# 3x3 convs one after the other on VectorE, read from PSUM, in a hybrid SSD and ConvFFN layer

## The chip, the cores and the metric

The kernel runs on one core of a Trainium2 chip. The core has TensorE for matmuls (PE in the profile, PEld for its weight loads), VectorE (DVE), ScalarE (ACT), GpSimd (POOL) and SyncE (SP), which here issues the DMAs. Matmul results land in PSUM; SBUF holds everything else. The metric is the device time of one execution in microseconds, lower is better.

## What is computed

One layer of a diffusion backbone runs over 640 tokens: 512 latent tokens, which form a grid of 8 rows by 64, and 128 context tokens. The model width is 1024. First comes a token mixer (a bidirectional state-space scan beside a 31-tap conv, one output projection), then a gated ConvFFN, where the change lies:

```python
h = rms_norm(x, prm["norm_ffn_pre"]) * (1 + sc2) + sh2
up = h @ prm["w_ffn_up"]                       # 1024 -> 5632
# context: width-3 conv along the sequence; latent: 3x3 conv on the grid, depthwise
up = dwconv1d(...) if rows is None else dwconv2d(up, prm["w_ffn_conv"], prm["b_ffn_conv"], rows)
f_gate, f_val = jnp.split(up, 2, axis=-1)
f = (jax.nn.silu(f_gate) * f_val) @ prm["w_ffn_down"]   # 2816 -> 1024
x = x + g2 * rms_norm(f, prm["norm_ffn_post"])
```

All arrays are float32.

## The kernel before

Activations lie transposed: 128 channels on the partitions, the 640 tokens along the free dimension, so that a tile is 128 x 640. Float32 matmuls are made of three products: weight and activation are each split into a rounded part (`hi`) and the rest (`lo`), and `mm3` (L267) adds hi x hi, hi x lo and lo x hi. Each product takes two matmuls, of 384 and 256 columns, so that one chunk of 128 output channels, with 8 blocks of 128 input channels, is 48 matmuls. Weights come by DMA in units of 512 KB (`fetch`), ScalarE writes their `hi` (L165) and GpSimd their `lo` (L167), two units ahead; there are three buffers for each part.

The up projection has 44 chunks. Number i stands for pair q = i // 2 and its half, gate (even) or value (odd). A chunk's sums fill one of three PSUM buffers in turn (`next_ps`), so that a chunk can start only when the one three before has been read to its end. Reading it is the conv, `up_conv`: ScalarE writes centre tap plus bias into a slot in SBUF (L1069), and VectorE adds the eight other grid taps (L1079, 441, 448 or 504 elements by tap) and the two taps of the context tokens (L1081, L1082; 127 elements), ten instructions that each read and write the same slot. When both halves of a pair are done, `finish(q)` applies SiLU to the gate (ScalarE, L1155) and multiplies it with the value (GpSimd; L1157 for the first four pairs, which are split into hi and lo at once, L253 and L255, and L1161 for the others, which are kept whole in the slots of `FRAW`). When the last chunk's matmuls are done, `split_f` splits what was kept (L253 on ScalarE, L255 on VectorE), into the slots of `ht`, some of which held the up projection's own input until then. The down projection follows.

The first five chunks, the head, are special. The activations come in two column ranges, 0 to 383 early and 384 to 639 late (`all_h2`). Chunks 0, 1 and 2 take their first range into the three PSUM buffers; chunks 3 and 4 take theirs into the free part of two of these, and ScalarE copies it to SBUF (L1104, `raws`, slots H5 and H6). When the second range is there, the order is 0, 3, 4, 1, 2 (L1101); chunks 3 and 4 are again copied to SBUF.

In the kernel before, six chunks (1, 2, 5, 6, 15 and 16; the table `EV`) are copied by ScalarE from PSUM to SBUF as soon as they are there (L1131), and their conv reads the copy, so that the PSUM buffer is free after the copy. The convs of chunks 3 and 4, from SBUF too, come behind those of chunks 8 and 14.

The framework orders each engine's instructions when the program is built, by a simulation of the timeline with priority by program order; each engine then works through its list in that order and waits on semaphores. Two instructions on one engine can therefore be swapped or mixed where the simulation saw the earlier one wait. `tc.issue_after(ins)` keeps what is traced inside it behind `ins` on the engine of `ins`. In the kernel before it binds the convs of chunks 0, 1 and 2 to one order, and those of 3 and 4 behind their forerunners; the others are free.

Of the kernel before, what the change touches and what calls it, by code (L numbers as in the profile page):

```python
# [9 lines left out]
AF = mybir.ActivationFunctionType  # L10
# [7 lines left out]
T = L + C  # L18
# [3 lines left out]
KD = D // P  # L22
# [7 lines left out]
NF = DFF // P  # L30
# [17 lines left out]
def hybrid_layer_kernel(ctx: ExitStack, tc: tile.TileContext, xT, ct, prm, cst, wrest, wdt, idhl_d, wada1, wada2, win,  # L48
                        wout, wup, wdown, st0, yT, nsf, nsb):
    nc = tc.nc  # L50
    te, ve, ac, gp, sy = nc.tensor, nc.vector, nc.scalar, nc.gpsimd, nc.sync
# [81 lines left out]
    def fetch(upto):  # L133
        if horizon[0] is not None:
            upto = min(upto, horizon[0])
        while cursor[0] < len(units) and cursor[0] <= upto:
            j = cursor[0]
            src, _ = units[j]
            n = src.shape[1]
            t = wp.tile([P, 1024], F32, tag="wr", name=f"wr{j}", bufs=2)  # L140
            sy.dma_start(t[:, :n], src)
            loaded[j] = t
            cursor[0] += 1
            split_unit(j)

    def get_unit(i):
        fetch(i + AHEAD)
        return ready.pop(i)
# [86 lines left out]
    ups = [(q, half) for q in range(NF) for half in range(2)]  # L235
# [25 lines left out]
    def mm3(pt, hi, lo, j, xh, xl, first, last, halves=(0, 1)):  # L261
        w1 = hi[:, j * P:(j + 1) * P]
        w2 = lo[:, j * P:(j + 1) * P]
        for i, (w, x) in enumerate(((w1, xh), (w1, xl), (w2, xh))):
            for h in halves:
                o, c0, c1 = HALF[h]
                last_mm[0] = te.matmul(pt[:, o:o + c1 - c0], w, x[:, c0:c1], start=first and i == 0, stop=last and i == 2)  # L267
# [28 lines left out]
    def ada_load(i, tags):  # L296
        ws = []
        for kc, tag in enumerate(tags):
            t = slot(tag)
            sy.dma_start(t[:, 0:4 * P], wada2[i, kc])  # L300
            ws.append(t)
        return ws

    def ada_half(i, ws):
        pt = psq(i % 2)
        for kc, w in enumerate(ws):
            for j in range(4):
                te.matmul(pt[32 * j:32 * j + 32, 0:P], cts[:, kc, :], w[:, j * P:(j + 1) * P],
                          start=kc == 0, stop=kc == KD - 1, tile_position=(0, 32 * j))
        r = sm.tile([P, P], F32, tag="adar", name=nm("adar"), bufs=1)  # L310
        ac.activation(r, pt[:, 0:P], AF.Copy)
        b = 8 * ADA_REST[i // 2] + 4 * (i % 2)
        ada_out(r, pt, P, (b, b + 1, b + 2, b + 3))
# [457 lines left out]
    for it in seq:  # L771
        if it[0] == "proj":
            n = it[1]
            pt = proj(n)
# [86 lines left out]
    prior = None  # L861
    for p in range(NA, NPAIR):
        for h in range(2):
            with tc.issue_after(prior.ins) if prior else nullcontext():
                prior = ve.scalar_tensor_tensor(tp[p][:, h * HT:(h + 1) * HT], tp[p][:, h * HT:(h + 1) * HT],
                                                prm_col("ssd_g", p), pry[h][:, 0:HT], MUL, MUL)
# [11 lines left out]
    def next_ps():  # L878
        rot[0] += 1
        return psum(rot[0] % 3)  # L880
# [169 lines left out]
    for half in range(2):  # L1050
        for m in range(OUT_FULL, KD):
            pt = next_ps()
# [14 lines left out]
    def up_conv(v, i, out):  # L1067
        w = lambda a, b: prm_col("ffn_w", 9 * i + 3 * a + b)
        ac.activation(out, v, AF.Identity, bias=prm_col("ffn_b", i), scale=w(1, 1))  # L1069
        vl = v[:, 0:L].rearrange("p (r c) -> p r c", c=GW)  # L1070
        ol = out[:, 0:L].rearrange("p (r c) -> p r c", c=GW)
        for a in range(3):
            for b in range(3):
                if (a, b) == (1, 1):
                    continue
                r0, r1 = max(0, 1 - a), min(ROWS, ROWS + 1 - a)
                q0, q1 = max(0, 1 - b), min(GW, GW + 1 - b)
                ob = ol[:, r0:r1, q0:q1]
                ve.scalar_tensor_tensor(ob, vl[:, r0 + a - 1:r1 + a - 1, q0 + b - 1:q1 + b - 1],  # L1079
                                        w(a, b), ob, MUL, ADD)  # L1080
        ve.scalar_tensor_tensor(out[:, L + 1:T], v[:, L:T - 1], w(1, 0), out[:, L + 1:T], MUL, ADD)  # L1081
        return ve.scalar_tensor_tensor(out[:, L:T - 1], v[:, L + 1:T], w(1, 2), out[:, L:T - 1], MUL, ADD)  # L1082
# [8 lines left out]
    head = [next_ps() for i in range(3)]  # L1091
    raws = {i: slot(f"H{2 + i}") for i in range(3, HEAD)}
# [5 lines left out]
    def up_mm(i, k, half, pt, o):  # L1098
        (hi, lo), (c0, c1) = ws[i], HC[half]
        for j, (w, x) in enumerate(((hi, h2[k][0]), (hi, h2[k][1]), (lo, h2[k][0]))):  # L1100
            te.matmul(pt[:, o:o + c1 - c0], w[k] if i in (1, 2) else w[:, k * P:(k + 1) * P], x[:, c0:c1],  # L1101
                      start=k == 0 and j == 0, stop=k == KD - 1 and j == 2)
        if k == KD - 1 and i >= 3:
            ac.activation(raws[i][:, c0:c1], pt[:, o:o + c1 - c0], AF.Copy)  # L1104
# [17 lines left out]
    conved = {}  # L1122


    EV = {1: "S14", 2: "S15", 5: "S6", 6: "S7", 15: "S14", 16: "S15"}

    def up_conv_of(i, v, out):
        conved[i] = out
        if i in EV:
            raw = slot(EV[i])  # L1130
            ac.activation(raw, v, AF.Copy)  # L1131
            v = raw
        return up_conv(v, ups[i][1] * NF + ups[i][0], out)

    acc_slot = lambda q, half: slot({(1, 0): "S16", (2, 1): "S17"}.get((q, half), f"S{10 + 2 * half + q % 2}"))
    ada_half(6, ada_w2)
    prior = None
    for i in (0, 3, 4, 1, 2):
        if i >= 3:
            pt = psq((i + 1) % 2)  # L1140
            for k in range(KD):
                up_mm(i, k, 1, pt, 0)
            horizon[0] += 1
            fetch(horizon[0])
            continue
        with tc.issue_after(prior.ins) if prior else nullcontext():
            for k in range(KD):
                up_mm(i, k, 1, head[i], 512)
            prior = up_conv_of(i, view(head[i]), acc_slot(*ups[i]))
    horizon[0] = None  # L1150
    FRAW = [f"H{i}" for i in (2, 3, 4, 7, 0, 5, 1, 6, 8, 9, 10, 11, 12, 13, 14, 15)] + ["S8", "S9"]

    def finish(q):
        a, b = conved.pop(2 * q), conved.pop(2 * q + 1)
        ac.activation(a, a, AF.Silu)  # L1155
        if q < NDIR:
            gp.tensor_tensor(a, a, b, MUL)  # L1157
            f_hl[q] = split_act(f"S{2 * q}", f"S{2 * q + 1}", a, gp)
        else:
            f_raw[q] = slot(FRAW[q - NDIR])  # L1160
            gp.tensor_tensor(f_raw[q], a, b, MUL)  # L1161

    finish(0)
    for i in range(HEAD, 2 * NF):
        q, half = ups[i]
        w = get_unit(unit_of["up", i])
        pt = next_ps()
        for k in range(KD):
            mm3(pt, *w, k, *h2[k], k == 0, k == KD - 1)
        if i == 2 * NF - 1:  # L1170
            break
        prior = up_conv_of(i, view(pt), acc_slot(q, half))
        if half and q > 2:
            finish(q)
        if i in (8, 14):
            j = 3 if i == 8 else 4
            with tc.issue_after(prior.ins):
                up_conv_of(j, raws[j], slot(f"H{j - 3}"))
            finish(j // 2)
        if i == 11:  # L1180
            with tc.issue_after(last_mm[0].ins):
                ada_half(7, ada_w2)
        if i == 5:
            ada_w2 = ada_load(7, [f"H{8 + k}" for k in range(8)])


    ht = ([(f"T{i}", f"T{8 + i}") for i in range(8)] + [("H2", "H3"), ("H4", "H7"), ("H0", "H5"), ("H1", "H6")]
          + [(f"S{i}", f"S{i + 1}") for i in (10, 12, 14)] + [(f"H{i}", f"H{i + 1}") for i in (8, 10, 12)])
    def split_f(q):
        f_hl[q] = split_act(*ht[q - NDIR], f_raw[q], ve)  # L1190

# [8 lines left out]
    gg2 = sb.tile([P, KD, 2], F32, tag="asc", name="gg2")  # L1200
    ve.tensor_tensor(gg2, modv[:, 40:48, :], prm_col("g_ffn_post", 0, 8).unsqueeze(2).to_broadcast([P, 8, 2]), MUL)
    msq = sb.tile([P, T], F32, tag="ysq", name="m2sq")
    mtags = ["H14", "H15", "S8", "S9", "S16", "S17", "U0", "U1"]
    mg = [None] * KD
    def down_mm(m, half, pt, ks):
        halves = BOTH if half is None else (half,)
# [61 lines left out]
    for m in range(2, KD - 1):  # L1268
        pt = next_ps()
# [4 lines left out]
    pt = next_ps()  # L1274
    down_mm(m, 0, pt, range(NF))
    down_out(m, 0, pt)
    pt = next_ps()
# [131 lines left out]
```

## Time and profile before

| | |
|---|---|
| median of three runs | 1042.57 us (1042.2 to 1050.46) |
| profiled execution, device time | 1052.25 us |
| profiled execution, span | 1050.5 us |
| granted TensorE clock, mean over the span | 0.979 |
| busy: PE, DVE, POOL, ACT | 94%, 73%, 55%, 42% |
| up chunks after the head | 575.4 to 876.3 us of the span |

How to read the lines below. A row of a group gives the line, the engine and the operation, output <- inputs (`ps` and `pq` are PSUM tiles, `S`, `H`, `T` slots in SBUF, `wr`, `wh`, `wl` the raw, hi and lo weights, `prms` the table of parameters), shapes and count, then busy time in us and mean ns of one, then the idle time of the engine ahead of these instructions and what ended most of it. A row of the timeline has the start and the time taken in us, merged over the count at its end, and in brackets the idle time ahead and its releaser. A row of the waits says who waited for whom: us in total, times, the longest. A row of the windows has the stretch, its length, and for PE, PEld, DVE, ACT and POOL the busy us and the instructions, then the granted TensorE clock, the share of the DMA engines and GB/s.

### The profile page before, as it was taken

What the parts mean: (1) busy time and instruction counts of PE and PEld (TensorE: products, weight loads), DVE (VectorE), ACT (ScalarE), POOL (GpSimd) and SP (SyncE); (2) the same over time, 40 slices, a digit from 0 to 9 for tenths busy, and PEclk for the clock granted to TensorE, in tenths of its full rate; (3) what the DMA queues carried; (4) which work ended last, traced back from release to release, by engine and by line L of the source; (5) the groups of instructions that cost most, each with busy time, mean ns of one, the idle gap of its engine ahead of it and who ended that gap; (6) DMA issues with size and microseconds to landing.
All of it is one profiled execution on the core that took longest, in us unless ns stands there. A gap on an engine that the chain in (4) does not pass through costs nothing. (4 is left out here: it accounts for less than half of the span.)

```text
span 1050.5 us, 18797 instructions
## 1 busy us (share of the span) xinstructions
PE 985.3 (94%) x7655; PEld 950.9 (91%) x7655; DVE 767.6 (73%) x1125; ACT 442.8 (42%) x740; POOL 573.5 (55%) x402
## 2 busy tenths in 40 slices
PE   5999999999999899799989968989999999999996
PEld 2799999999899789799879968989999999999995
DVE  3789999989999988942585999998888889300004
ACT  6244648556365676423455422333233235222221
POOL 3333978879769875443662434574443444344444
PEclk9999999999999999899999989999999999899998
DMA  9622221222111122478462311221222222132212
GB/s 346 221 66 76 66 71 61 71 75 69 60 61 48 36 59 80 159 268 287 134 210 96 118 41 61 61 80 61 81 67 75 81 63 68 56 88 65 71 54 101
DMA packets 42934, 102.76 MB, mean 98 GB/s; under 512 B 4832, under 2 KB 12768, under 8 KB 42848
## 3 DMA queue, kind: packets, MB, share of 16 engines
q1 hardware_dynamic: 42848, 101.56, 29.8%
q8 instruction: 60, 0.98, 0.4%
q14 instruction: 26, 0.21, 0.1%
HBM read 97.87 MB, written 3.67 MB: 97 GB/s over the span
## 5 line engine op out<-in xcount | busy, mean ns | idle before, releaser
L167 POOL TENSOR_TENSOR wl<-wr,wh 128x1024 fp32r<-128x1024 f32 (+3 forms) x127 | 301.2, 2373 | 318.2 <-ACT wh L165 312.2
L267 PE MATMUL ps<-H,wh 128*128 128x384 f32 (+1 forms) x1664 | 327.1, 310 | 4.9 <-DVE M L413 2.2
L267 PE MATMUL ps<-T,wh 128*128 128x384 f32 (+1 forms) x1504 | 287.9, 312 | 17.8 <-DVE S L1082 17.7
L165 ACT ACTIVATE wh<-wr 128x1024 fp32r<-128x1024 f32 (+3 forms) x131 | 131.7, 1005 | 351.2 <-PE ps L267 232.1
L267 PEld LDWEIGHTS ps<-H,wh 128*128 128x128 f32 x1664 | 253.3, 188 | 9.0 <-issue 4.3
L267 PEld LDWEIGHTS ps<-T,wh 128*128 128x128 f32 x1504 | 229.8, 190 | 18.7 <-issue 18.4
L1079 DVE SCALAR_TENSOR_TENSOR S<-ps,prms,S 128x441 f32<-128x441 f32 (+2 forms) x288 | 197.4, 693 | 34.3 <-ACT S L1069 28.0
L713 DVE SCALAR_TENSOR_TENSOR ps<-u,prms,ps 128x655 f32<-128x655 f32 x223 | 200.8, 901 | 9.9 <-ACT ps L710 5.4
L267 PE MATMUL ps<-H,wl 128*128 128x384 f32 (+1 forms) x832 | 198.1, 310 | 0.0
L267 PE MATMUL ps<-T,wl 128*128 128x384 f32 (+1 forms) x752 | 174.3, 311 | 0.0
L267 PEld LDWEIGHTS ps<-H,wl 128*128 128x128 f32 x832 | 130.8, 188 | 1.8 <-issue 1.4
L267 PEld LDWEIGHTS ps<-T,wl 128*128 128x128 f32 x752 | 117.1, 190 | 0.0
L333 DVE RECIPROCAL rsm<-rsm 128x160 f32<-128x160 f32 (+2 forms) x9 | 7.3, 815 | 143.8 <-ACT rsm L332 143.8
L267 PE MATMUL ps<-S,wh 128*128 128x384 f32 (+1 forms) x448 | 96.4, 323 | 7.5 <-DVE S L1082 3.2
L267 PEld LDWEIGHTS ps<-S,wh 128*128 128x128 f32 x448 | 73.6, 197 | 10.0 <-issue 5.9
L267 PE MATMUL ps<-S,wl 128*128 128x384 f32 (+1 forms) x224 | 58.7, 315 | 0.3 <-POOL wl L167 0.3
L629 ACT ACTIVATE S<-pq,ACM 128x128 f32<-128x128 f32 x140 | 40.9, 372 | 18.3 <-PE pq L623 18.1
L1079 DVE SCALAR_TENSOR_TENSOR S<-S,prms,S 128x441 f32<-128x441 f32 (+2 forms) x48 | 46.0, 988 | 1.4 <-ACT S L1069 1.3
L267 PEld LDWEIGHTS ps<-S,wl 128*128 128x128 f32 x224 | 38.1, 193 | 0.5 <-POOL wl L167 0.5
L1069 ACT ACTIVATE S<-ps,prms 128x640 f32<-128x640 f32 x36 | 31.3, 868 | 0.0
L1161 POOL TENSOR_TENSOR H<-S,S 128x640 f32<-128x640 f32 x16 | 25.5, 1594 | 3.9 <-DVE S L1082 3.8
L580 POOL TENSOR_TENSOR S<-S,stmp 128x128 f32<-128x128 f32 x36 | 18.6, 517 | 15.1 <-ACT S L569 11.2
(345 smaller groups left out, 1245.1 us busy)
## 6 DMA issues: line engine op xcount, KB each, us to landing
wr<-in_wup SPq DMA_DIRECT2D x44, 512.0 KB, 3.4
wr<-in_win SPq DMA_DIRECT2D x36, 512.0 KB, 3.4
T<-in_wada SPq DMA_DIRECT2D x49, 256.0 KB, 5.4
wr<-in_wdown SPq DMA_DIRECT2D x16, 512.0 KB, 3.5
wr<-in_wout SPq DMA_DIRECT2D x13, 512.0 KB, 3.5
H<-in_wada SPq DMA_DIRECT2D x23, 256.0 KB, 5.1
S<-in_wada SPq DMA_DIRECT2D x16, 256.0 KB, 5.7
wr<-in_wdown SPq DMA_DIRECT2D x8, 384.0 KB, 3.1
```

The lines of the kernel that those rows point to most:

```text
L165: ac.activation(hi[:, :n], raw[:, :n], AF.Copy)
L167: lo_eng.tensor_tensor(lo[:, :n], raw[:, :n], hi[:, :n].bitcast(F32), SUB)
L267: last_mm[0] = te.matmul(pt[:, o:o + c1 - c0], w, x[:, c0:c1], start=first and i == 0, stop=last and i == 2)
L333: ve.reciprocal(r[:, 0:seg], r[:, 0:seg])
L580: gp.tensor_tensor(now, now, tmp, ADD)
L629: ac.activation(r[:, c * P:(c + 1) * P], pb[:, (c - c0) * P:(c - c0 + 1) * P], AF.Relu, scale=-1.0, bias=ACM[:, c, row:row + 1])
L713: ve.scalar_tensor_tensor(acc, u[:, j:j + UO], w(j), acc, MUL, ADD)
L1069: ac.activation(out, v, AF.Identity, bias=prm_col("ffn_b", i), scale=w(1, 1))
L1079: ve.scalar_tensor_tensor(ob, vl[:, r0 + a - 1:r1 + a - 1, q0 + b - 1:q1 + b - 1], w(a, b), ob, MUL, ADD)
L1161: gp.tensor_tensor(f_raw[q], a, b, MUL)
```

## The change

`EV` and its copies go: every conv reads its chunk from PSUM, but for chunks 3 and 4, whose sums lie in `raws`. Every conv's VectorE instructions are now kept behind the last one of the conv traced before it, all through the 44 chunks. The convs of chunks 3 and 4 come behind those of 18 and 28 (before: 8 and 14) and write to S8 and S9 (before: H0 and H1). As H5 and H6 stay taken for longer, the slots of the kept products, of their splits and of two output tiles are dealt out anew. The ring of PSUM buffers, the matmuls, the weights and the DMAs are the same.

```diff
-    EV = {1: "S14", 2: "S15", 5: "S6", 6: "S7", 15: "S14", 16: "S15"}
+    LATE = {18: (3, "S8"), 28: (4, "S9")}
+    prior = [None]
 
     def up_conv_of(i, v, out):
         conved[i] = out
-        if i in EV:
-            raw = slot(EV[i])
-            ac.activation(raw, v, AF.Copy)
-            v = raw
-        return up_conv(v, ups[i][1] * NF + ups[i][0], out)
+        with tc.issue_after(prior[0].ins) if prior[0] else nullcontext():
+            prior[0] = up_conv(v, ups[i][1] * NF + ups[i][0], out)
...
-        with tc.issue_after(prior.ins) if prior else nullcontext():
-            for k in range(KD):
-                up_mm(i, k, 1, head[i], 512)
-            prior = up_conv_of(i, view(head[i]), acc_slot(*ups[i]))
+        for k in range(KD):
+            up_mm(i, k, 1, head[i], 512)
+        up_conv_of(i, view(head[i]), acc_slot(*ups[i]))
     horizon[0] = None
-    FRAW = [f"H{i}" for i in (2, 3, 4, 7, 0, 5, 1, 6, 8, 9, 10, 11, 12, 13, 14, 15)] + ["S8", "S9"]
+    FRAW = [f"H{i}" for i in (2, 3, 4, 7, 0, 1, 8, 9, 10, 11, 12, 13, 14, 15, 5, 6)] + ["S8", "S9"]
...
-        prior = up_conv_of(i, view(pt), acc_slot(q, half))
+        up_conv_of(i, view(pt), acc_slot(q, half))
         if half and q > 2:
             finish(q)
-        if i in (8, 14):
-            j = 3 if i == 8 else 4
-            with tc.issue_after(prior.ins):
-                up_conv_of(j, raws[j], slot(f"H{j - 3}"))
+        if i in LATE:
+            j, to = LATE[i]
+            up_conv_of(j, raws[j], slot(to))
             finish(j // 2)
...
-    ht = ([(f"T{i}", f"T{8 + i}") for i in range(8)] + [("H2", "H3"), ("H4", "H7"), ("H0", "H5"), ("H1", "H6")]
-          + [(f"S{i}", f"S{i + 1}") for i in (10, 12, 14)] + [(f"H{i}", f"H{i + 1}") for i in (8, 10, 12)])
+    ht = ([(f"T{i}", f"T{8 + i}") for i in range(8)] + [("H2", "H3"), ("H4", "H7"), ("H0", "H1"), ("H8", "H9")]
+          + [(f"S{i}", f"S{i + 1}") for i in (10, 12, 14)] + [(f"H{i}", f"H{i + 1}") for i in (10, 12, 14)])
...
-    mtags = ["H14", "H15", "S8", "S9", "S16", "S17", "U0", "U1"]
+    mtags = ["H5", "H6", "S8", "S9", "S16", "S17", "U0", "U1"]
```

More of the change, by code (lines that the diff above doesn't have):

```diff
@@ L1122, in hybrid_layer_kernel @@
     conved = {}
-    EV = {1: "S14", 2: "S15", 5: "S6", 6: "S7", 15: "S14", 16: "S15"}
+    LATE = {18: (3, "S8"), 28: (4, "S9")}
+    prior = [None]
     def up_conv_of(i, v, out):
         conved[i] = out
-        if i in EV:
-            raw = slot(EV[i])
-            ac.activation(raw, v, AF.Copy)
-            v = raw
-        return up_conv(v, ups[i][1] * NF + ups[i][0], out)
+        with tc.issue_after(prior[0].ins) if prior[0] else nullcontext():
+            prior[0] = up_conv(v, ups[i][1] * NF + ups[i][0], out)
     acc_slot = lambda q, half: slot({(1, 0): "S16", (2, 1): "S17"}.get((q, half), f"S{10 + 2 * half + q % 2}"))
     ada_half(6, ada_w2)
-    prior = None
     for i in (0, 3, 4, 1, 2):
```

## The prediction

> **What bounds the kernel now.** I read the page first: which engine is busiest, and what two kinds of 3x3 conv cost (line L1079 reads the conv's input from PSUM, "ps", or from SBUF, "S").
>
> ```profile
> span 1050.5 us, 18797 instructions
> PE 985.3 (94%) x7655; PEld 950.9 (91%) x7655; DVE 767.6 (73%) x1125; ACT 442.8 (42%) x740; POOL 573.5 (55%) x402
> ...
> L167 POOL TENSOR_TENSOR wl<-wr,wh 128x1024 fp32r<-128x1024 f32 (+3 forms) x127 | 301.2, 2373 | 318.2 <-ACT wh L165 312.2
> ...
> L1079 DVE SCALAR_TENSOR_TENSOR S<-ps,prms,S 128x441 f32<-128x441 f32 (+2 forms) x288 | 197.4, 693 | 34.3 <-ACT S L1069 28.0
> ...
> L1079 DVE SCALAR_TENSOR_TENSOR S<-S,prms,S 128x441 f32<-128x441 f32 (+2 forms) x48 | 46.0, 988 | 1.4 <-ACT S L1069 1.3
> ```
>
> TensorE is the bound, so only its idle time can be won. The view of waits, for TensorE from 600 us on, and its timeline say where that idle time lies in the stage the change touches; the windows give the granted clock around it (the figure after the five engines' busy times).
>
> ```profile
> PE ps L267 <- DVE S L1082: 20.9, 4, 10.2
> ```
> ```profile
> 620.25 1.41 PE L267 MATMUL ps<-T,wh 128*128 128x384 f32 x4 [10.19 <-DVE S L1082]
> 640.42 1.41 PE L267 MATMUL ps<-T,wh 128*128 128x384 f32 x4 [2.90 <-DVE S L1082]
> 702.02 1.41 PE L267 MATMUL ps<-T,wh 128*128 128x384 f32 x4 [4.65 <-DVE S L1082]
> 893.77 1.41 PE L267 MATMUL ps<-S,wh 128*128 128x384 f32 x4 [3.19 <-DVE S L1082]
> ```
> ```profile
> 620.00:640.00 20.00, 17.27 (x160) 16.84 (x160) 19.93 (x30) 5.42 (x7) 10.23 (x5) 0.92 0.19 55
> 640.00:660.00 20.00, 19.58 (x126) 19.60 (x127) 18.50 (x36) 5.78 (x7) 11.11 (x6) 0.91 0.15 53
> ...
> 700.00:720.00 20.00, 17.98 (x111) 18.01 (x112) 17.27 (x32) 4.98 (x6) 9.38 (x6) 0.91 0.24 79
> ```
>
> Four times TensorE waits for the last instruction of a conv (L1082), that is for VectorE to give a PSUM buffer back. Each wait leaves a slow clock behind it: 20 us at 0.92, 0.91 and 0.91 is 1.6, 1.8 and 1.8 us more. The first three waits cost 10.19 + 2.90 + 4.65 + 5.2 = 22.9 us. The fourth belongs to the splits after the last chunk, which the change leaves as they are.
>
> VectorE is late in the first three because of the convs from SBUF, which the change takes out:
>
> ```profile
> L1079 DVE SCALAR_TENSOR_TENSOR S<-ps,prms,S 128x441 f32<-128x441 f32 x30 | 19.8, 672 | 2.7 <-ACT S L1069 2.3
> L1079 DVE SCALAR_TENSOR_TENSOR H<-H,prms,H 128x441 f32<-128x441 f32 x8 | 9.3, 1167 | 0.0
> ```
> ```profile
> 580.90 0.66 DVE L1079 SCALAR_TENSOR_TENSOR S<-S,prms,S 128x441 f32<-128x441 f32 x1
> 583.20 10.91 DVE L1079 SCALAR_TENSOR_TENSOR S<-S,prms,S 128x504 f32<-128x504 f32 x12
> 594.03 2.50 DVE L1081 SCALAR_TENSOR_TENSOR S<-S,prms,S 128x127 f32<-128x127 f32 x1
> ```
> ```profile
> 588.98 1.90 POOL L1157 TENSOR_TENSOR S<-S,S 128x640 f32<-128x640 f32 x1 [9.60 <-ACT S L1131]
> 590.84 5.55 POOL L167 TENSOR_TENSOR wl<-wr,wh 128x1024 fp32r<-128x1024 f32 x2
> ```
>
> Undisturbed, an SBUF instruction takes 0.66 us, the same as one from PSUM (0.672). But while GpSimd works in SBUF (588.98 to 596), a 127-column one takes 2.50: VectorE with two SBUF inputs and GpSimd take turns. A conv from PSUM has one SBUF input and shows no such stretch.
>
> **The change part by part.** *Removed: six ScalarE copies (chunks 1, 2, 5, 6, 15, 16).* ScalarE is 42% busy, so their own time is worth nothing; they freed PSUM early, and that is lost. *Added: one conv after the other, from PSUM.* What does one cost alone?
>
> ```profile
> 570.56 5.81 DVE L1079 SCALAR_TENSOR_TENSOR S<-ps,prms,S 128x441 f32<-128x441 f32 x8 [5.01 <-ACT S L1069]
> 576.29 0.34 DVE L1081 SCALAR_TENSOR_TENSOR S<-ps,prms,S 128x127 f32<-128x127 f32 x1
> 576.66 0.35 DVE L1082 SCALAR_TENSOR_TENSOR S<-ps,prms,S 128x127 f32<-128x127 f32 x1
> ...
> 614.68 4.26 DVE L1079 SCALAR_TENSOR_TENSOR S<-ps,prms,S 128x504 f32<-128x504 f32 x7
> 618.85 0.34 DVE L1081 SCALAR_TENSOR_TENSOR S<-ps,prms,S 128x127 f32<-128x127 f32 x1
> ```
>
> Chunk 0's conv runs alone from 570.56 to 577.01: 6.4 us from one conv to the next. Where two are mixed, seven instructions take 4.17 us (614.68 to 618.85), 0.60 each against 0.72 alone, so mixed a conv would be about 5.4: strict order costs 1.0 us per conv there. It costs next to nothing in the later chunks, which already run one by one (0.72 per instruction).
>
> [...] The rows just shown differ, 0.72 against 0.60, and the sum goes by the rows.
>
> TensorE's pace, and when a conv can start, from ScalarE's queue (L165 splits weights once a chunk's matmuls end; L1069 is the conv's bias pass):
>
> ```profile
> 655.84 1.06 ACT L165 ACTIVATE wh<-wr 128x1024 fp32r<-128x1024 f32 x1 [4.42 <-PE ps L267]
> 656.80 0.87 ACT L1069 ACTIVATE S<-ps,prms 128x640 f32<-128x640 f32 x1
> 662.72 1.06 ACT L165 ACTIVATE wh<-wr 128x1024 fp32r<-128x1024 f32 x1 [3.24 <-PE ps L267]
> ...
> 725.01 1.06 ACT L165 ACTIVATE wh<-wr 128x1024 fp32r<-128x1024 f32 x1 [3.62 <-PE ps L267]
> ...
> 739.41 1.06 ACT L165 ACTIVATE wh<-wr 128x1024 fp32r<-128x1024 f32 x1 [3.62 <-PE ps L267]
> ```
> ```profile
> 664.59 0.68 DVE L1079 SCALAR_TENSOR_TENSOR S<-ps,prms,S 128x441 f32<-128x441 f32 x1 [0.68 <-ACT S L1069]
> ```
>
> A chunk takes TensorE 6.88 us here (655.84 to 662.72); 6.4 is less, so VectorE keeps up by 0.5 us per chunk. In rhythm a conv starts 1.9 us after its matmuls end (664.59 less 662.72), is done at 8.3, and its buffer is wanted two chunks later, at 13.8: 5.4 us to spare.
>
> The head, worked forward: conv 0 ends at 577.0, so chunk 5 starts there and not at 575.4 (before, TensorE took up the buffer of chunk 1, copied out by then): a loss of 1.7. Convs 1 and 2 end at 583.3 and 589.7, chunk 5's at 596.1; chunks 6, 7 and 8 want these buffers at 583.9, 590.8 and 597.6. All are in time, the last by 1.5 us, and the spare grows by 0.5 per chunk until it is full near chunk 13. So all three waits go: 22.9 - 1.7 = **21.2 us won**.
>
> *Moved: the two convs from SBUF, now behind chunks 18 and 28.* Queued behind each on VectorE is the next chunk's conv, and behind that the PSUM buffer for three chunks later. Below, such a conv is 6.4 us if no GpSimd instruction meets it; above, the excess of the H row (1.167 against 0.672, 0.5 on each of eight) gives 10.4. I work it out: GpSimd's weight split (2.37 us) comes once in 6.88 us, one is under way when the conv starts (about 2 us to wait) and another falls into it: 6.4 + 2.0 + 2.3 = 10.7. I take 10.7, near the H rows. Counting from the end of chunk 18's matmuls, conv 19 is then done at 8.3 + 10.7 + 6.4 = 25.4 and wanted at 3 x 6.88 = 20.6: TensorE waits 4.8 us, plus 1.7 of slow clock, as after the 4.65 us wait. By chunk 28 nine chunks have restored the spare (9 x 0.5, and 1.7), so the same again: 2 x 6.5 = **13.0 us lost**.
>
> *Slots and the rest.* New places for outputs, products and splits have as many instructions and bytes as before; the DMA queue gets the same loads. I cost them at nothing: the rhythm's 5.4 us to spare hides a slot that comes free late, and what goes beyond it would come on top one for one.
>
> Sum: 21.2 - 13.0 = 8.2 us less. On the profiled execution 1052.25 us becomes 1044.1. That execution is 9.7 above the median of 1042.57. After its third wait a chunk takes 7.2 us (725.01 to 739.41 is two), 0.32 more on 24 chunks or 7.7 us; the runs shown, 1042.2 to 1050.46, differ by about as much. I take it that the median run kept 6.88 throughout, and the forecast is 1042.57 - 8.2 = **1034.4 us**.
>
> **The rivals.** *Late convs nearly hidden* (6.4 to 8.5 us each): waits of 0.5 to 2.6 us, with or without a slow clock, 1022 to 1030. For:
>
> ```profile
> 677.67 14.23 POOL L167 TENSOR_TENSOR wl<-wr,wh 128x1024 fp32r<-128x1024 f32 x2 [4.47 <-ACT wh L165]
> ```
>
> Here two SBUF convs mixed held GpSimd off, 14.23 us for two splits, and VectorE went on. Against: that was the dense order, 0.60 per instruction; at 0.72 GpSimd can get in between.
>
> *The slow pace comes early.* If after the wait at chunk 22 the pace is 7.2, 21 chunks cost 6.7 and the second wait is 0.7 shorter: 1040.4. For: it happened after a 4.65 us wait. Against: not after two others.
>
> *VectorE sets the pace: slower than before.* The first down-projection matmul shows when chunk 43 ended before:
>
> ```profile
> 876.26 0.76 PE L267 MATMUL ps<-S,wh 128*128 128x384 f32 x4
> ```
>
> That is 868.6 in a run at 6.88 throughout (7.7 less). If every conv also waits 0.68 us for its bias pass, as at 664.59, the chain steps by 7.1. From 570.6, with 39 steps and two late convs (21.4), conv 40 ends at 868.9 and chunk 43, which needs its buffer, 6.9 later at 875.8: 7 us more than before, 1050. This rival decides from 6.9 us per conv. Against: with a backlog the bias passes lie ready, and the rhythm above has room. [...]
>
> *The change does only half of what it says.* Strict order binds VectorE's convs alone; where ScalarE and GpSimd stand is still the builder's choice. If a head conv's bias pass is queued behind a late instruction and half of the first wait stays, 5.1 and 1.7 us, the time is 1041, 1037 to 1043 with the late convs' spread.
>
> **How the numbers follow.** Forecast with late convs of 8.5 to 12 us, 1030 to 1038: 0.45. Nearly hidden: 0.17. Slow pace: 0.15. Half of what it says: 0.08. VectorE sets the pace: 0.15, two thirds of it above 1053, where further waits add slow clocks. About 1% is what a measurement here tells from no change: faster below 1032.1 (the hidden case and two fifths of the forecast), 0.35; slower above 1053, 0.10; the rest 0.55. A range of 1024 to 1048 leaves out some 0.2.
>
> **What would show it.** Right: no wait on L1082 before chunk 20; two waits of 3 to 6 us about 68 us apart, each behind a group S<-H of ten instructions lasting 9 to 12 us; convs 6.4 us apart in the head. Wrong: a wait in the head (chain over 6.9), none behind the late convs, or 7.2 us chunks from the start, 12.5 us in all.

## The result

The changed kernel takes 1039.43 us (median; 1036.45 to 1044.49), the kernel before 1043.47 us (1039.01 to 1051.72) beside it. The ratio is 0.9949, with a 95% interval of 0.9929 to 0.9969: a gain of 5.3 us, within the 1% that was named as the bound of "no change". The forecast was 1034.4 us, 8.2 less than before, in a range of 1024 to 1048. The direction and the range held, the time is 5 us off, and two terms of the sum were wrong by nearly as much as the whole gain, in opposite directions, so that it is in part luck that the sum came near.

The page of the changed kernel, first its span (the profiled execution took 1039.19 us):

```profile
span 1037.4 us, 18797 instructions
PE 979.7 (94%) x7655; PEld 944.8 (91%) x7655; DVE 756.7 (73%) x1125; ACT 438.7 (42%) x734; POOL 565.6 (55%) x402
```

VectorE's groups of line L1079, by what the conv reads:

```profile
L1079 DVE SCALAR_TENSOR_TENSOR S<-ps,prms,S 128x441 f32<-128x441 f32 (+2 forms) x336 | 233.2, 694 | 19.9 <-ACT S L1069 10.2
L1079 DVE SCALAR_TENSOR_TENSOR S<-H,prms,S 128x441 f32<-128x441 f32 (+2 forms) x16 | 16.6, 1036 | 0.0
```

336 of the 352 grid instructions now read PSUM, at 694 ns as before (693). The 16 that are left from SBUF take 1036 on average: still 0.34 more than the others, since some of them still meet GpSimd: the first one of conv 3, at 685.23 us, takes 2.67 us beside a weight split that runs from 685.02 for 2.41 us. TensorE now waits four times for a conv's last instruction:

```profile
576.80 0.82 PE L267 MATMUL ps<-T,wh 128*128 128x384 f32 x4 [1.87 <-DVE S L1082]
700.60 1.04 PE L267 MATMUL ps<-T,wh 128*128 128x384 f32 x4 [2.76 <-DVE S L1082]
775.58 0.82 PE L267 MATMUL ps<-T,wh 128*128 128x384 f32 x4 [1.27 <-DVE S L1082]
866.87 1.40 PE L267 MATMUL ps<-S,wh 128*128 128x384 f32 x4 [8.26 <-DVE S L1082]
```

These are chunk 5, chunk 22, chunk 32 and the first matmul of the down projection. The windows give the granted clock (the figure after the five engines) of 20 us around or behind each of the four, and then that of the kernel before around its fourth wait, at 893.77. That one stands inside the down projection: its first matmul came at 876.26 without a wait, and the wait is ahead of its second tile of 128 channels.

```profile
570.00:590.00 20.00, 18.13 (x124) 17.96 (x123) 18.91 (x32) 10.80 (x14) 11.85 (x6) 0.91 0.42 143
700.00:720.00 20.00, 19.40 (x119) 19.43 (x120) 19.11 (x33) 5.51 (x7) 12.09 (x7) 0.91 0.17 53
775.00:795.00 20.00, 19.42 (x135) 19.45 (x136) 19.12 (x33) 6.93 (x10) 13.44 (x7) 1.00 0.21 67
866.00:886.00 20.00, 19.13 (x115) 19.16 (x116) 17.82 (x27) 5.27 (x7) 7.34 (x4) 0.86 0.11 35
```
```profile
892.00:912.00 20.00, 18.23 (x105) 18.26 (x106) 9.17 (x14) 3.27 (x4) 4.66 (x4) 0.83 0.18 54
```

The three waits of before (10.19, 2.90 and 4.65 us) are gone. In their place: 1.8 us of later start and 1.8 of slow clock at chunk 5 (0.91, where the kernel before had 1.00 in the same 20 us); 2.76 + 1.8 and 1.27 + 0 behind the two late convs; and where the kernel before waited 3.19 us ahead of the second tile of the down projection, the changed one waits 8.26 ahead of the first. With the slow clock (20 us at 0.86 is 2.8, at 0.83 it is 3.4) that is 11.1 us against 6.6, or 4.5 more than before. The balance: 22.9 - 3.6 - 5.8 - 4.5 = 9.0 us.

The rest is TensorE's own pace, which the starts of ScalarE's weight splits show, one a chunk, as in the prediction:

```profile
649.48 1.06 ACT L165 ACTIVATE wh<-wr 128x1024 fp32r<-128x1024 f32 x1 [3.35 <-PE ps L267]
656.31 1.06 ACT L165 ACTIVATE wh<-wr 128x1024 fp32r<-128x1024 f32 x1 [4.99 <-PE ps L267]
...
716.45 1.06 ACT L165 ACTIVATE wh<-wr 128x1024 fp32r<-128x1024 f32 x1 [5.37 <-PE ps L267]
723.65 1.06 ACT L165 ACTIVATE wh<-wr 128x1024 fp32r<-128x1024 f32 x1 [3.27 <-PE ps L267]
```

Up to chunk 21 a chunk takes about 6.9 us (656.31 less 649.48 is 6.83, and two steps are 13.76), from chunk 22 to 31 it is 7.20, and from chunk 32 on 6.88 again. Ten chunks at 0.32 more are 3.2 us, so 9.0 becomes 5.8, against 5.3 measured. From profile to profile the spans differ by 13.1 us, because the profiled execution of before ran 24 chunks at 7.20 (7.7 us): 9.0 + 7.7 - 3.2 = 13.5.

### The profile page after: what moved, and what is told of

Read it like the earlier page. It is cut to its first block, busy times and chain, and to the rows that moved or that the text cites. A ratio compares the mean times of both kernels' runs of the same rounds, so it can differ in the third digit from the quotient of the medians.

```text
span 1037.4 us, 18797 instructions
## 1 busy us (share of the span) xinstructions
PE 979.7 (94%) x7655; PEld 944.8 (91%) x7655; DVE 756.7 (73%) x1125; ACT 438.7 (42%) x734; POOL 565.6 (55%) x402
## 4 chain that ended last, share of the span: by engine, by line
PE 75%; DVE 13%; issue 3%; ACT 3%; POOL 3%; DMA 2%; SPq 0%; POOLq 0%; ACTq 0%; DVEq 0%
PE ps L267 64%; DVE S L1079 4%; PE ps L1101 2%; PE pq L308 2%; POOL wl L167 1%; PE pq L658 1%; DVE T L752 1%; PE pq L647 1%; DVE ps L713 1%; PE pq L565 1%; DMA wr<-in_wout 1%; PE pq L289 1%; DMA T<-in_xT 1%; PE pq L623 1%; ACT wh L165 1%
## 5 line engine op out<-in xcount | busy, mean ns | idle before, releaser
L167 POOL TENSOR_TENSOR wl<-wr,wh 128x1024 fp32r<-128x1024 f32 (+3 forms) x127 | 294.5, 2320 | 333.9 <-ACT wh L165 327.7
L267 PE MATMUL ps<-T,wh 128*128 128x384 f32 (+1 forms) x1504 | 283.9, 310 | 5.9 <-DVE S L1082 5.9
L1079 DVE SCALAR_TENSOR_TENSOR S<-ps,prms,S 128x441 f32<-128x441 f32 (+2 forms) x336 | 233.2, 694 | 19.9 <-ACT S L1069 10.2
L267 PEld LDWEIGHTS ps<-T,wh 128*128 128x128 f32 x1504 | 227.3, 189 | 7.0 <-ACT wh L165 3.5
L267 PEld LDWEIGHTS ps<-S,wh 128*128 128x128 f32 x448 | 73.7, 197 | 15.2 <-issue 11.2
L1069 ACT ACTIVATE S<-ps,prms 128x640 f32<-128x640 f32 x42 | 36.5, 868 | 0.0
L580 POOL TENSOR_TENSOR S<-S,stmp 128x128 f32<-128x128 f32 x36 | 18.6, 517 | 15.0 <-ACT S L569 11.2
L1152 ACT ACTIVATE S<-S 128x640 f32<-128x640 f32 x22 | 16.1, 732 | 24.3 <-DVE S L1082 24.3
```

The source lines that it names most:

```text
L167: lo_eng.tensor_tensor(lo[:, :n], raw[:, :n], hi[:, :n].bitcast(F32), SUB)
L580: gp.tensor_tensor(now, now, tmp, ADD)
```

## The experiments

The labels are those by which the expectations name the kernels; there is no e7 and no e10. All times are medians beside the kernel before on the same chip (1043.5 to 1043.8), ratios are to it. Differences between two ratios have an interval worked out as the root of the sum of squares of their half widths. Where a step's line number is a few higher than in the kernel before (L1084 for L1082, L1101 for L1082), lines were inserted above it.

### One part of the change at a time

Three kernels each take one part alone. **All convs from PSUM** (e1), free order, late convs behind 8 and 14:

```diff
-    EV = {1: "S14", 2: "S15", 5: "S6", 6: "S7", 15: "S14", 16: "S15"}
+    EV = {}
```

> The kernel before with the table EV empty: every chunk's conv but those of chunks 3 and 4 reads PSUM, the order stays free and the convs of chunks 3 and 4 stay behind 8 and 14. Theory (the convs from SBUF make the first waits, the place of the late convs the others): the 10.2 us wait at chunk 10 goes, but conv 3 now comes where VectorE has no spare yet, so a wait of some 7 us stays near chunk 12 and one of 3 to 5 us near chunk 18, each with 1.7 us of slow clock; 22.9 less 1.7 less 8.7 less 6.5 is 6 us won, ratio about 0.994. Rival (the strict order carries the gain): a wait of about 10 us in the head stays, ratio 0.998 to 1.002.

Measured: 1041.96 us, 0.9991 (0.9954 to 1.0028). TensorE's timeline in this kernel:

```profile
597.15 0.82 PE L267 MATMUL ps<-T,wh 128*128 128x384 f32 x4 [2.68 <-DVE S L1082]
635.93 0.82 PE L267 MATMUL ps<-T,wh 128*128 128x384 f32 x4 [2.24 <-DVE S L1082]
685.42 1.41 PE L267 MATMUL ps<-T,wh 128*128 128x384 f32 x4 [6.23 <-DVE S L1082]
```

The 10.2 us wait is gone, so the convs from SBUF did make it. The waits that replace it, 11.2 us in all beside 1.88 at chunk 5, are as large as expected, but at chunks 7, 12 and 18, and not at 12 and 18 alone. The trace has 5 us less of waits and slow clock than before, near the 6 expected, but the ratio shows no gain: its interval lies above the expected 0.994. Its times lie between 1037 and 1051, as the two paces below would spread them.

**Strict order alone** (e2; copies and late places as before):

```diff
-        return up_conv(v, ups[i][1] * NF + ups[i][0], out)
+        with tc.issue_after(last[0].ins) if last[0] else nullcontext():
+            last[0] = up_conv(v, ups[i][1] * NF + ups[i][0], out)
+        return last[0]
```

> The kernel before with every conv's VectorE instructions kept behind the last one of the conv traced before it; the six copies and the places of the late convs stay. Theory (strict order by itself costs, 0.72 us an instruction in place of 0.60, and the convs from SBUF stay): the first wait grows from 10.2 to about 18 us, 8 convs by 1.0 us each, and the others stay; some 1050 us, ratio 1.007. Rival (strict order carries the gain, since a conv that runs alone ends sooner than two that are mixed): the first wait shrinks by 5 us or more, ratio 0.995 or less.

Measured: 1054.13 us, 1.0085 (1.0049 to 1.012). Slower, as the theory had it, but not for its reason:

```profile
617.07 1.41 PE L267 MATMUL ps<-T,wh 128*128 128x384 f32 x4 [8.40 <-DVE S L1082]
...
880.97 1.41 PE L267 MATMUL ps<-S,wh 128*128 128x384 f32 x4 [8.25 <-DVE S L1082]
```

The first wait fell to 8.40 (10.19 before) instead of growing to 18; the second and third are 3.21 and 5.86 (2.90 and 4.65 before). What grew most is the wait at the down projection, 8.25 ahead of its first tile where the kernel before has 3.19 ahead of its second, as in the changed kernel.

**Late places alone** (e3; convs of chunks 3 and 4 behind 18 and 28, new slots, all else as before):

```diff
-        if i in (8, 14):
-            j = 3 if i == 8 else 4
+        if i in LATE:
+            j, to = LATE[i]
             with tc.issue_after(prior.ins):
-                up_conv_of(j, raws[j], slot(f"H{j - 3}"))
+                up_conv_of(j, raws[j], slot(to))
```

> The kernel before with the convs of chunks 3 and 4 behind 18 and 28 and the slots dealt out as in the changed kernel; copies and free order stay. Theory: the first wait of 10.2 us stays, since chunk 10 waits for convs ahead of that of chunk 3; the second (2.9 and 1.8 us of clock) goes, and the two late convs bring 3 to 7 us in their new places; -3 to +2 us, ratio 0.997 to 1.002. Rival (the late convs in the head made the backlog): the first wait shrinks too, 6 us or more won, ratio 0.994 or less.

Measured: 1052.08 us, 1.0059 (1.0033 to 1.0084), slower than either theory had it. The first wait stayed at 10.17, but the late convs cost waits of 6.18 and 4.17 us, more than in the changed kernel; the first of the two:

```profile
715.62 1.41 PE L267 MATMUL ps<-T,wh 128*128 128x384 f32 x4 [6.18 <-DVE S L1082]
```

At the down projection it waits 3.32 us, and the first kernel of the three 3.31, both ahead of the second tile: the two free orders keep that wait as it was, the strict order has 8.25 ahead of the first.

No part gains anything alone; the ratios of the three add up to 1.35% slower, and together they are 0.5% faster. The parts need each other: without the convs from SBUF there is room for late convs, and without a strict order, below, the PSUM convs still wait.

### The wait ahead of the down projection

VectorE's timeline in the changed kernel, from the start of chunk 41's conv, and then the same place in the kernel before:

```profile
850.21 3.67 DVE L1079 SCALAR_TENSOR_TENSOR S<-ps,prms,S 128x441 f32<-128x441 f32 x5
854.65 1.86 DVE L255 TENSOR_TENSOR T<-H,T 128x640 fp32r<-128x640 f32 x2 [0.77 <-ACT T L253]
856.43 0.67 DVE L1079 SCALAR_TENSOR_TENSOR S<-ps,prms,S 128x441 f32<-128x441 f32 x1
...
865.65 0.81 DVE L255 TENSOR_TENSOR H<-H,H 128x640 fp32r<-128x640 f32 x1
866.38 0.34 DVE L1082 SCALAR_TENSOR_TENSOR S<-ps,prms,S 128x127 f32<-128x127 f32 x1
```
```profile
871.46 0.34 DVE L1082 SCALAR_TENSOR_TENSOR S<-ps,prms,S 128x127 f32<-128x127 f32 x1
871.72 1.51 DVE L255 TENSOR_TENSOR T<-H,T 128x640 fp32r<-128x640 f32 x1
...
893.29 0.33 DVE L1082 SCALAR_TENSOR_TENSOR S<-ps,prms,S 128x127 f32<-128x127 f32 x1
```

Before, the splits (L255) begin when conv 41 has ended (871.46). They stand among the taps of conv 42, which runs from 870.87 to 893.29, and the wait at 893.77 is for that conv's buffer, which the second down tile takes. In the changed kernel they have moved one conv forward: they stand after five of the eight grid taps of conv 41, some waiting for ScalarE (L253), and its last instruction comes at 866.38, 16 us after its first. The first down matmul needs that PSUM buffer and starts at 866.87. The remedy (e4) keeps them behind the conv of chunk 42 (`ends` holds each conv's last grid tap and last context tap):

```diff
     for q in range(NDIR, EARLY):
-        split_f(q)
+        with tc.issue_after(ends[42][0].ins), tc.issue_after(ends[42][1].ins):
+            split_f(q)
```

> The changed kernel with the splits after the last chunk (all but those of the first four pairs) kept on VectorE behind the whole conv of chunk 42. Theory (the wait ahead of the down projection grew from 3.2 to 8.5 us because splits, which wait for ScalarE, were queued in the middle of conv 41 on VectorE, whose PSUM buffer the first down matmul needs): the wait falls to 2 to 3 us; 5 to 8 us less than the changed kernel, 1031 to 1034 us where the kernel before takes 1042.6, ratio 0.989 to 0.992. Rival (VectorE is simply 3.6 us behind at the end, and what is not waited for here is waited for a tile later): waits of 6 us or more stay in the first two down tiles, within 2 us of the changed kernel, ratio 0.994 to 0.997.

Measured: 1029.55 us, 0.9838 (0.9798 to 0.9878), 11.6 us (give or take 4.7) below the changed kernel. The same place on VectorE now, the last one being the splits:

```profile
854.51 5.80 DVE L1081 SCALAR_TENSOR_TENSOR S<-ps,prms,S 128x441 f32<-128x441 f32 x8
860.23 0.34 DVE L1083 SCALAR_TENSOR_TENSOR S<-ps,prms,S 128x127 f32<-128x127 f32 x1
860.61 0.35 DVE L1084 SCALAR_TENSOR_TENSOR S<-ps,prms,S 128x127 f32<-128x127 f32 x1
860.88 5.96 DVE L255 TENSOR_TENSOR T<-H,T 128x640 fp32r<-128x640 f32 x8
```

TensorE waits for a conv neither ahead of the first nor of the second down tile, which is more than was expected. The same edit to the **kernel before** (e9):

> The kernel before with the splits after the last chunk kept on VectorE behind the whole conv of chunk 42, as was done to the changed kernel in e4. Theory (the wait ahead of the down projection was 3.2 us and 3.4 us of slow clock in the kernel before, and is worth no more there): 3 to 6.5 us less than before, ratio 0.994 to 0.997; with both mended the change is then worth 10 to 14 us. Rival (the place of the splits is worth the same in both kernels, so that e4 has nothing to do with the change): ratio 0.988 to 0.990.

Measured: 1039.47 us, 0.9958 (0.9931 to 0.9985), or 4.4 us. TensorE does not wait at the down projection here either. So the splits' place was worth 4.4 us before, in conv 42, and 11.6 after, in conv 41, and with it mended in both kernels the change is worth 0.9958 - 0.9838, 12.5 us (give or take 5.0).

Why did the splits get into conv 41? VectorE had fallen 3.6 us behind by then; is it that, or their place in its list? Two kernels ask. In the first (e6), **the late convs do nothing on VectorE** (their ten taps are left out, and with them part of the result):

```diff
-            up_conv_of(j, raws[j], slot(to))
+            conved[j] = slot(to)
+            ac.activation(conved[j], raws[j], AF.Identity, bias=..., scale=...)
```

> The changed kernel with the VectorE work of the convs of chunks 3 and 4 left out (their eight grid taps and two context taps are not computed; ScalarE still writes centre tap and bias). It prices the late convs. Theory (each late conv makes one wait, and VectorE's 3.6 us of delay at the end, left over from them, lets the splits get into the middle of conv 41): no wait at chunks 22 and 32, 6.5 us less, and the wait ahead of the down projection back at 3 to 4 us, 4.5 less: 1028 to 1030, ratio 0.985 to 0.988. Rival (the splits' place in VectorE's list makes that wait by itself): it stays above 6 us, 1032 to 1034, ratio 0.989 to 0.992.

In the second (e13), **the split of pair 18**, over which VectorE stalls 3.2 us in the middle of conv 38, is kept behind conv 42. The edit is that of above on the loop over the last six pairs (16 to 21); of their splits, only that of pair 18 stood ahead of conv 41:

> The changed kernel with only the split of pair 18 kept behind conv 42, the others as they are. In the changed kernel VectorE stalls 3.2 us for it in the middle of conv 38 and is 3.6 us late from there on. Theory (the wait ahead of the down projection comes of the splits that stand in the middle of conv 41, in VectorE's list, as the run without the late convs said): it stays at 8 us, and the time within 2 us of the changed kernel, ratio 0.993 to 0.997. Rival (VectorE's lateness from that stall makes it): the wait falls by 3 us or more, 1034 to 1037 us, ratio 0.989 to 0.993.

Measured: 1031.64 us, 0.9879 (0.9843 to 0.9915), and 1037.06 us, 0.9923 (0.9889 to 0.9957). The first down matmul in the one and in the other:

```profile
859.90 1.41 PE L267 MATMUL ps<-S,wh 128*128 128x384 f32 x4 [7.91 <-DVE S L1082]
```
```profile
869.73 1.41 PE L267 MATMUL ps<-S,wh 128*128 128x384 f32 x4 [7.91 <-DVE S L1084]
```

The wait stays at 7.9 us without the late convs and without the stall. In the second kernel VectorE is not late at all, since it stands idle ahead of conv 41 until the bias pass is done:

```profile
849.03 3.67 DVE L1081 SCALAR_TENSOR_TENSOR S<-ps,prms,S 128x441 f32<-128x441 f32 x5 [0.68 <-ACT S L1071]
```

So VectorE's lateness does not make the wait. The theory that it did, which the first of the two stated, fell; the place in the list makes it. It is the waits that decide here; the times alone would have spoken for the theory that fell: 0.9879 lies at the end of its range in the first, and 0.9923, 2.7 us (give or take 4.1) below the changed kernel, within it in the second. The first kernel also prices the late convs, at 7.3 us (give or take 4.3) in the changed kernel. The splits' place goes with the strict order: every kernel with that order and with free splits (the changed one, the strict order alone, these two, and the truly strict one below) waits 7.9 to 8.3 us ahead of the first down tile, and every one with a free order and free splits (the kernel before, all convs from PSUM alone, the places alone) 3.2 to 3.3 ahead of the second. The new slots do not make it, since the strict order alone has the old ones and the places alone the new ones. Why the builder of the list deals the splits out so is open.

### The late convs

The changed kernel's bond is on the last context tap, which does not depend on the grid taps, so that the next conv may start before the late one is done. Here (e5) each conv is bound behind **both last taps** of its forerunner (`grid` holds the last grid tap):

```diff
-        with tc.issue_after(prior[0].ins) if prior[0] else nullcontext():
+        with tc.issue_after(prior[0].ins) if prior[0] else nullcontext(), tc.issue_after(grid[0].ins) if grid[0] else nullcontext():
```

> The changed kernel with each conv kept behind both the last grid tap and the last context tap of the conv before it, so that no two convs mix on VectorE. Theory (the late convs cost half of what was forecast because the changed kernel's bond lets conv 3 mix with conv 19 and conv 4 with conv 29: 15.1 us for both in place of 10.7 + 6.4 = 17.1): the waits at chunks 22 and 32 grow from 3.0 and 1.6 to about 4.8 us each, and each has its slow clock, so 5 to 8 us more than the changed kernel, 1044 to 1047, ratio 1.000 to 1.004. Rival (mixing saves nothing, a late conv simply meets fewer weight splits than forecast): waits as in the changed kernel, within 2 us of it, ratio 0.994 to 0.997.

Measured: 1045.50 us, 1.0006 (0.9978 to 1.0033), 5.9 us (give or take 3.5) above the changed kernel. VectorE's timeline around conv 3, in the changed kernel and in this one, where it is S<-H:

```profile
685.23 2.67 DVE L1079 SCALAR_TENSOR_TENSOR S<-H,prms,S 128x441 f32<-128x441 f32 x1
687.83 0.34 DVE L1081 SCALAR_TENSOR_TENSOR S<-H,prms,S 128x127 f32<-128x127 f32 x1
688.09 0.67 DVE L1079 SCALAR_TENSOR_TENSOR S<-H,prms,S 128x448 f32<-128x448 f32 x1
688.69 0.34 DVE L1082 SCALAR_TENSOR_TENSOR S<-H,prms,S 128x127 f32<-128x127 f32 x1
688.95 0.66 DVE L1079 SCALAR_TENSOR_TENSOR S<-ps,prms,S 128x441 f32<-128x441 f32 x1
...
700.10 0.35 DVE L1082 SCALAR_TENSOR_TENSOR S<-ps,prms,S 128x127 f32<-128x127 f32 x1
```
```profile
686.37 2.67 DVE L1081 SCALAR_TENSOR_TENSOR S<-H,prms,S 128x441 f32<-128x441 f32 x1
...
690.09 6.55 DVE L1081 SCALAR_TENSOR_TENSOR S<-H,prms,S 128x441 f32<-128x441 f32 x6
696.55 5.80 DVE L1081 SCALAR_TENSOR_TENSOR S<-ps,prms,S 128x441 f32<-128x441 f32 x8
```

Truly alone, conv 3 takes 10.2 us (686.37 to 696.55) and conv 4 as much: 10.7 was the forecast. In the changed kernel its context taps come second and fourth of its ten instructions, conv 19 starts at 688.95, 3.7 us into conv 3, and both together take 15.1 us (685.23 to 700.37) where one after the other takes 16.6 (10.2 and 6.4). TensorE's waits in the truly strict kernel are then near the 4.8 us of the forecast:

```profile
703.14 1.40 PE L267 MATMUL ps<-T,wh 128*128 128x384 f32 x4 [4.17 <-DVE S L1084]
779.19 1.41 PE L267 MATMUL ps<-T,wh 128*128 128x384 f32 x4 [4.17 <-DVE S L1084]
```

If it is the one piece that hurts, the ten instructions can be **dealt out singly**, each behind another chunk's conv. On top of the edit that keeps the splits behind conv 42 (e8):

```diff
-    LATE = {18: (3, "S8"), 28: (4, "S9")}
+    LATE = {8: (3, "S8"), 23: (4, "S9")}
+    SPREAD = (0, 1, 3, 4, 6, 7, 9, 10, 12, 13)
...
+        for s in LATE:
+            if i - s in SPREAD:
+                with tc.issue_after(prior[0].ins), tc.issue_after(grid[0].ins):
+                    prior[0] = next(taps[s])
+                if i - s == SPREAD[-1]:
+                    finish(LATE[s][0] // 2)
```

> As e4, and the ten VectorE instructions of each late conv are dealt out one at a time behind the convs of ten chunks (those of conv 3 between chunks 8 and 21, of conv 4 between 23 and 36). Theory (a late conv makes a wait only because it comes in one piece, longer than the 5.4 us that a buffer has to spare): one instruction of 0.7 to 2.5 us a chunk is hidden, no wait at all between chunk 5 and the down projection; e4 less its two waits of 3.0 us and their 5.1 us of slow clock, 1018 to 1021 us, ratio 0.974 to 0.979. Rival (VectorE has too little time to spare per chunk, 0.5 us, and the waits only come in other places): one or more waits of 2 us or over on the conv's last instruction, within 4 us of e4, ratio 0.980 to 0.988.

Measured: 1022.25 us, 0.9788 (0.9754 to 0.9822): no wait at chunk 22 or 32, one of 1.7 us at chunk 41 and one of 0.75 ahead of the first down tile. Against the kernel with the splits behind conv 42 alone (e4) that is 5.2 us less, give or take 5.5, so the time alone does not settle it; the missing waits do. The wait at chunk 41 follows a stall of VectorE in the middle of conv 38, for the split of pair 18, which was still free:

```profile
827.72 2.25 DVE L255 TENSOR_TENSOR S<-H,S 128x640 fp32r<-128x640 f32 x1 [3.88 <-ACT S L253]
```

With **this split bound as well** (e12; again the loop over the last six pairs):

> As e8, and the one split that e8 left free (that of pair 18, whose slots S14 and S15 are free once the table EV is gone) is kept behind conv 42 too. It stood in the middle of conv 38, where VectorE waited 3.9 us for ScalarE. Theory (that stall makes e8's last wait, 1.9 us at chunk 41): no wait on a conv's last instruction from chunk 6 to the down projection, 1.9 us less than e8: 1018 to 1022 us, ratio 0.975 to 0.979. Rival (VectorE is short of time at the end anyway): a wait of 1 us or more stays at chunks 41 to 43, ratio 0.978 to 0.982.

Measured: 1018.03 us, 0.9743 (0.9707 to 0.9779), the best of all, by the ratios 26.8 us below the kernel before and 21.5 (give or take 4.3) below the changed one.

```profile
span 1016.6 us, 18809 instructions
PE 972.4 (96%) x7655; PEld 937.5 (92%) x7655; DVE 753.8 (74%) x1125; ACT 438.0 (43%) x734; POOL 567.2 (56%) x402
```

The waits at chunk 41 and at the down projection are gone. From 600 us to the end of the down projection TensorE does not wait for VectorE's convs at all; what is left of such waits is 1.87 us at chunk 5.

### What the strict order is worth

As the kernel with the splits behind conv 42 (e4), but **free in order** from chunk 5 on (e11):

```diff
-        with tc.issue_after(prior[0].ins) if prior[0] else nullcontext():
+        with tc.issue_after(prior[0].ins) if prior[0] and i in (1, 2, 3, 4) else nullcontext():
```

> As e4 (all convs from PSUM, late convs behind 18 and 28, splits behind conv 42), but the strict order is kept for the convs of chunks 1 to 4 alone; the others are free. It prices the strict order by itself, where there is no conv from SBUF in its way. Theory (each conv's end frees a PSUM buffer, so two convs that are mixed free the first one's buffer late; with all convs from PSUM free in order there was a 2.7 us wait at chunk 7): that wait comes back, with or without 1.7 us of slow clock, and the rest stays: 1031 to 1035 us, ratio 0.987 to 0.992. Rival (mixing makes convs denser, 0.60 us an instruction in place of 0.72, so the free order is as good): within 2 us of e4, ratio 0.982 to 0.986.

Measured: 1035.91 us, 0.9904 (0.9874 to 0.9935), 6.9 us (give or take 5.2) more than with the strict order.

```profile
594.46 0.83 PE L267 MATMUL ps<-T,wh 128*128 128x384 f32 x4 [2.68 <-DVE S L1084]
...
780.51 1.40 PE L267 MATMUL ps<-T,wh 128*128 128x384 f32 x4 [4.17 <-DVE S L1084]
```

The wait at chunk 7 is back, as the theory said, and the waits at chunks 22 and 32 are 4.27 and 4.17 us where the strict kernel with the same splits has 2.76 and 2.77. The view puts the one at chunk 22 down to a ScalarE split, but the last tap of conv 19, which that chunk's buffer waits for, ended within 0.1 us of it, at 705.84.

## Why the prediction was right, and where it was wrong

**TensorE bound, three waits on L1082 made by the convs from SBUF: right.** The waits are gone in the changed kernel. The first one goes when the copies alone go (10.19 to no wait at chunk 10), and stays at 8.40 and 10.17 where the copies stay. The second and third go from their places when the late convs alone move (to none and 0.24).

**The head worked forward at 6.4 us per conv: right.** VectorE's timeline has the head's convs at an even step with nothing between:

```profile
576.58 5.80 DVE L1079 SCALAR_TENSOR_TENSOR S<-ps,prms,S 128x441 f32<-128x441 f32 x8
...
582.93 5.79 DVE L1079 SCALAR_TENSOR_TENSOR S<-ps,prms,S 128x441 f32<-128x441 f32 x8
...
589.29 5.80 DVE L1079 SCALAR_TENSOR_TENSOR S<-ps,prms,S 128x441 f32<-128x441 f32 x8
```

The step is 6.36 us. So the rival by which VectorE sets the pace, from 6.9 on, is out. Chunk 5 starts 1.8 us later against its conv 0 than before (576.80 less 570.21 against 575.37 less 570.56); 1.7 was forecast. What was left out is that this wait, too, can drop the clock: 1.8 us more here (0.91 over 20 us) and about as much in e8 (four matmuls take up to 1.27 us behind it, 0.76 later), none in e4, e5, e11 and e12 (1.00) with the same wait. The sign "no wait on L1082 before chunk 20" also left it out, though its 1.7 us stood in the sum. One step of the working does not come out: from 1.5 us at chunk 8 and 0.5 more a chunk, the spare time would be full near chunk 16, not 13. Nothing hangs on it, as the late convs come behind chunk 18.

**The late convs: mis-sized, 13.0 us forecast, 5.8 in the trace.** The size of one, 10.7, was nearly right (10.2 alone), and the waits for truly strict convs too (4.8 forecast, 4.17 idle). The step that failed is "Counting from the end of chunk 18's matmuls, conv 19 is then done at 8.3 + 10.7 + 6.4": it took the order for strict, as the change is described, where the bond on the last context tap lets conv 19 start 3.7 us into conv 3. The slow clock, 1.7 at each, was 1.8 at one and nothing at the other. The 1.27 us at chunk 32 owes something to the slow pace of the ten chunks ahead of it, as the rival of that name had it: with the same late convs at 6.88 us a chunk the wait there is 2.77 (e4) and 2.10 (e13).

**"The fourth belongs to the splits after the last chunk, which the change leaves as they are": wrong.** No line that orders the splits is changed, but their place in VectorE's list is: in conv 41 instead of conv 42. The wait that they make grew by 5.1 us. The error was to take an order that is worked out anew with every build for a property of the lines of code. It cost 4.5 us, and the two errors, 7.2 won and 4.5 lost with 1.9 at the head, leave 9.0 where 8.2 was forecast. That they nearly cancel is luck.

**"I take it that the median run kept 6.88 throughout": plausible for before, silent on after.** In the 20 runs beside the changed kernel, the kernel before has times of 1039 to 1044.6 and, apart from them, of 1048.4 to 1051.7, which would fit 24 chunks at one pace or the other; later runs of it also lie between (1045.6 and 1047.3), so this is not shown. But the forecast then kept 6.88 for the changed kernel's median run as well, and left the slow pace to a rival. Its profiled run had 10 chunks at 7.20, 3.2 us, and its times gather around 1037, 1039.5 and 1042, as if the two stretches behind its late waits drew their pace each for itself. That is an argument from times and one profile, not shown. By it, 3.2 less the 0.8 of above is 2.4 of the 2.9 us by which the gain, 5.3 by the ratio, falls short of 8.2. Of the rest of the 5 us, 0.9 is that the kernel before takes 1043.47 and not 1042.57, and 1.3 that the two medians lie 4.0 us apart where the ratio gives 5.3.

**A strict order "costs 1.0 us per conv there": wrong in what it makes of it.** A mixed conv is denser (0.60 us an instruction in the kernel before, 0.72 alone), but the first of two mixed convs ends late, and TensorE waits for its end: with all convs from PSUM in free order (e1), conv 2, mixed with conv 5, runs from 585.97 to 597.00, 11.0 us in place of 6.4, and chunk 7 waits for it. A strict order is worth 6.9 us, give or take 5.2.

## What to carry to other kernels

Where a framework orders each engine's list when the program is built, an edit that only binds some instructions moves others that nobody touched: compare the lists around every wait on the path, not those of the edited lines alone, and bind what must not come between. For a ring of buffers the end of the first instruction group counts, not the density of two (here 11.0 us for the first of two mixed convs, 6.4 for one alone), so finish one before the next; and work that is longer than a buffer's spare time is hidden when it is dealt out in pieces shorter than that (here the waits of 2.76 and 2.77 us at chunks 22 and 32 went). Parts of a change that each lose alone (here +0.9% and +0.6%, and one near zero) can win together, so judge them by the waits that they leave and not by their single times.

## What was not expected of the hardware

**Two paces of the same matmuls at the same clock.** The changed kernel's windows over whole chunks before and after chunk 22:

```profile
716.00:766.00 50.00, 50.00 (x335) 50.00 (x335) 45.41 (x73) 15.46 (x18) 21.84 (x10) 1.00 0.23 72
640.00:690.00 50.00, 50.00 (x351) 50.00 (x350) 46.56 (x75) 15.54 (x18) 22.32 (x11) 1.00 0.26 83
```

Clock 1.00 and TensorE busy throughout in both, yet 335 matmuls in the one and 351 in the other. In this profile the pace changed where TensorE had stood still: it went to 7.20 us a chunk at the wait of chunk 22 and back to 6.88 at that of chunk 32. But such a wait is not needed: the last kernel of the late convs (e12) went from 7.20 back to 6.88 between chunks 11 and 12, where other matmuls and no wait stand, and e4 from 6.88 to 7.25 at chunk 41 after a gap of 0.1 us. Nor does a wait decide it: after the same wait of 4.65 us the kernel before went on at 7.20, and with its splits bound (e9) at 6.88. The kernel with the fewest waits (e12) has the narrowest times (1016.26 to 1019.4). What decides the pace is open.

**The clock dropped after a wait of 1.87 us in one kernel, and not after one of 1.88 us in another.** Ahead of chunk 5 the wait of 1.87 us went with 0.91 over 20 us in the changed kernel, and a wait of 1.88 us there with 1.00 in the one with the splits behind conv 42 (e4):

```profile
570.00:590.00 20.00, 18.12 (x132) 17.96 (x131) 19.11 (x32) 10.84 (x15) 10.62 (x6) 1.00 0.49 158
```

At chunk 22 a wait of 2.76 us went with 0.91 in the changed kernel and with 0.84 in e4, over 20 us each. What decides whether the clock drops, and how far, is open.
